# Hybrid parallel-group encoder block on one core: down's first weight slabs and the leftovers of gate and up change places, one norm and one sine chain are placed elsewhere

## The chip, the core and the metric

The kernel runs on one core of a Trainium2 chip. The metric is the device time of one execution in microseconds (us); lower is better. The times of before are those of three runs, of which the median, the lowest and the highest are given, and one more execution was recorded by the hardware profiler.

The engines by the profile's names: PE is TensorE's matmuls and PEld its weight loads, DVE is VectorE, ACT is ScalarE, POOL is GpSimd and SP is SyncE. POOL does next to no arithmetic here: it issues small transfers. SP issues the transfers that bring weights and inputs.

## The reference

One encoder block over a sequence of 256 tokens of width 2048, with a memory of 256 rows, all in f32:

```python
mem_n = rms_norm(mem, mem_norm_g)
h = rms_norm(x, norm_g[l, 0])
q, k, v, g, lr, u_f, u_h, u_s = jnp.split(h @ w_in[l], split_at, axis=-1)
y_a = gla_mixer(q, k, v, g, lr, ...)
y_b = rms_norm(fnet_mixer(u_f), grp_norm_g[l, 0])
filt = hyena_filters(feats, hy_ffn_w1[l], hy_ffn_b1[l], hy_ffn_w2[l], ...)
y_c = rms_norm(hyena_mixer(u_h, hy_conv_w[l], filt, hy_skip[l]), grp_norm_g[l, 1])
y_d = rms_norm(shortconv_mixer(u_s, sc_conv_w[l]), grp_norm_g[l, 2])
mix = jnp.concatenate([y_a, y_b, y_c, y_d], axis=-1)
x = x + mix @ w_out[l]
x = x + cross_attention(rms_norm(x, norm_g[l, 1]), mem_n, w_xq[l], w_xkv[l], w_xo[l])
x = x + swiglu(rms_norm(x, norm_g[l, 2]), w_gate_up[l], w_down[l])
return rms_norm(x, final_norm_g)
```

Each of the four mixers gives 512 of the 2048 columns of `mix`. The filters of the Hyena mixer come from a small network with two sines of 64 x 256 values. `swiglu` is `(silu(h @ w_gate) * (h @ w_up)) @ w_down` with 5632 inner columns; w_gate_up is 2048 x 11264 and w_down 5632 x 2048. These two products take the larger part of the time.

## The kernel before

**Products in three passes.** An f32 operand is split into a high part (rounded to the matmul's f32r type) and a low part (the rest). A product is high by high, low by high and high by low, so three matmuls stand where one would in plain f32. Lines L473, L474 and L475 are these three in gate, up and down, where the activations are the stationary operand and 512 columns of weights move; L422 and L423 are a pair of matmuls that does the same in the projections, with 512 and 256 moving columns.

**The stream of weights.** All weights lie in one array in the order of use, cut into slabs of 128 x 2048. SP loads a slab into a buffer `raw` (L124). Each slab has two halves of 128 x 1024. For each half ACT casts the high part `wh` (L144) and DVE subtracts to get the low part `wl` (L145). Half by half they go into pools of pairs: three buffers always, two more in gate and up (`wp2`, until the slab number `DOWN`, where down's weights begin), one more in down (`wp3`). So up to five halves, then four, are prepared ahead of their use. A slab's `raw` buffer comes free when its second half is done. One slab of down takes 24 matmuls.

**Units.** Part of gate, up and down is multiplied with seven products in place of eight (a scheme after Strassen). These parts, called units, need sums of operand blocks and of weight blocks, formed by DVE (L174 for the weights).

**Gate and up.** `mlp` (from L886) calls `gate_up`, which runs over 11 column groups j of 512 columns. At the end of each group the sums leave PSUM and `finish` (a background generator) applies silu, multiplies, transposes on DVE (`u`, L502) and stores the group to the HBM array `hidden` by eight transfers from POOL (L505). `fetch` loads `hidden` back, one row block k of 128 x 256 at a time, on POOL (L915) into buffers `tmp` (a pool of 11), and splits each into `f[k]`, the operand of down: a cast on ACT (L308) and a subtraction on DVE (L300). The row blocks are named by their number here: f14 is block 14 of 44. The tiles behind f are of several pools, so the trace shows them as `act`, `f` or others. `turn` transposes the residual x in 16 steps, each with one DVE transpose and four stores from POOL (`xrows`, L1050), and then loads it back in row form (`res`, L1054).

**The background.** `bg` is a queue of generators. Each `bg.poll()` between matmuls lets them issue some work, by an estimate of the engines' load; `bg.drain(x)` issues all that x has left at once. So the program order of all engines is the order in which Python issues instructions, and each engine works through its own in that order. A scheduler may move an instruction ahead where its inputs allow it; `mark` and `keep_place` pin a stretch to the place where it was issued. At the end of `gate_up` (L1036) three generators are drained one after the other: `end` (the last group's finish), `turned` and `early` (the fetch of f0 to f15).

**Down.** `Down` runs by a plan: first the 32 plain row blocks, in eight slabs of four blocks (`plain`, L1105), then six units of two row blocks each (`unit`, L1118) mixed with plain slabs of the second half of the columns. `ready(k)` steps the running fetch until row block k is split. `begin` (L1177) starts the second fetch, for f16 to f43, which loads six blocks ahead, and then runs the plan. The row blocks from 32 on are loaded as pairs for the units; `form` builds their sums (`e`, `s`).

**The projection behind the mixers.** `out_proj` multiplies the mixers' outputs with w_out in four parts, in the order of operands 8, 0, 4, 12 (Hyena, GLA, FNet, short convolution). Ahead of each of the last three parts it calls a function with n = 0, 1, 2, which drains the generator that makes that part's operands. `g_sc` is the norm of the short convolution: it spreads row factors over partitions with two matmuls (L398, `pm<-dgh` and `pm<-dgl`), copies the result (`rs`, L404), multiplies four tiles by it (L304) and splits them (L308, L300).

**The sine.** `sine` (L1303) is a chain of a dozen DVE operations on 64 x 256 values that reduces the argument, and one ACT sine at its end. It is called twice, for the two sine layers; the second result `hs` is the operand of the matmuls at L1400.

Of the kernel before, what the change touches and what calls it, by code (L numbers as in the profile page):

```python
# [27 lines left out]
FT = DFF // P  # L28
# [10 lines left out]
ROWS = ((0, 512), (704, 768), (880, 944), (NBLK - 48 * FT, NBLK))  # L39

LATE = 12

EARLY = 16

# [22 lines left out]
PLANS = down_plan()  # L67

DOWN = GU // 16 + 16 * DFF // 1024
# [201 lines left out]
class Block:  # L271
# [283 lines left out]
    def mixers(self):  # L555
# [77 lines left out]
        with tc.tile_pool(name="mid", bufs=1) as mid:  # L633
            self.dgp = mid
            gl = Gla(self, mid)
            with tc.tile_pool(name="hyp", bufs=1) as hyp, tc.tile_pool(name="k2", bufs=8) as k2:
                hy = Hyena(self, hyp, k2)

                mem0 = hy.piece()[:, 0:R + 16]
                nc.sync.dma_start(mem0, self.t["mem0"])  # L640
                self.bg.add(prepare(mid))

                for cols in ([0, 512], [1024], [1536]):
                    first = dict(parts=[[k] for k in range(KT)], before=start_m) if len(cols) > 1 else {}
                    for c, ps in zip(cols, self.gemm_rows("w_xkv", cols, h, **first)):
                        for r in range(2):
                            self.store_turned(self.kd[c:c + 512, r * P:(r + 1) * P], hy.piece(), ps[r][:, :])
                    if first:
                        for k in range(0, KT, 4):
                            self.load_x(k, 4)  # L650
                for hd in range(4):
                    for r, p in enumerate(self.gemm_rows("w_xkv", [D + hd * 512], h, start_x if hd == 3 else rows.append)[0]):
                        for c in range(2):
                            v, o = self.tmp(), (2 * hd + r) * 512 + c * R
                            nc.scalar.activation(v, p[:, c * R:(c + 1) * R], AF.Copy, scale=self.rcm[:, r:r + 1])
                            nc.gpsimd.dma_start(self.vd[:, o:o + R], v)
                self.bg.drain()

                def ev_u(i, p):
                    hy.feed(i, self.merge(p))  # L660
                    if i == 4:
                        self.bg.add(hy.convs())

                self.gemm("w_in", [UH + i * P for i in range(12)], h, ev_u)
                for r, p in enumerate(self.gemm_rows("w_in", [512], h, lambda k: k or low_rank())[0]):
                    nc.scalar.copy(gl.v[r], p)
                self.gemm("w_in", [256, 384, 0, 128], h, lambda i, p: gl.feed(i, self.merge(p)))
                self.gemm("w_in", scols[0:NSC], h, ev_s, narrow=True)
                self.bg.drain()

            with tc.tile_pool(name="glp", bufs=1) as glp:
                gl.open(glp)
                fn = Fnet(self, glp, act[20:24])
                g_gla = self.bg.add(gl.mix(act[4:8]))
                fn.feed(self.gemm_rows("w_in", [UF], h)[0])
                g_fn = self.bg.add(fn.mix(act[0:4], gl))
                self.gemm("w_in", scols[NSC:], h, lambda i, p: ev_s(i + NSC, p))
                g_sc = self.bg.add(self.group_norm(self.res[1], 2, act[20:24]))

                def ev_gate(i, p):  # L680
                    nc.scalar.activation(gl.gate[i], p[:, 0:R], AF.Silu)

                self.gemm("w_in", [1024 + i * P for i in range(4)], h, ev_gate, narrow=True)
                gl.done = True
                self.out_proj(lambda n: self.bg.drain((g_gla, g_fn, g_sc)[n]))

    def conv3(self, u, c, y=None):
        y = self.tmp() if y is None else y
# [188 lines left out]
    def mlp(self):  # L877
        tc, nc, act, st = self.tc, self.nc, self.act, self.st
        slots = lambda pool, n, a, b: [pool.tile([P, 512], F32R, name=f"{n}{i}") for i in range(a, b)]
        with tc.tile_pool(name="fp", bufs=1) as fp:  # L880
            self.gap(fp, 192)
            f = act[4:12] + slots(fp, "f", 8, EARLY)
            self.gap(fp, 64)
            with tc.tile_pool(name="wp2", bufs=2) as wp2, tc.tile_pool(name="rawx", bufs=1) as st.rawx, \
                    tc.tile_pool(name="sw", bufs=1) as sw, tc.tile_pool(name="gp", bufs=1) as gp:
                self.gap(sw, 192)  # L886
                st.pools.append([wp2, 2, DOWN])
                self.gate_up(sw, gp, f)
            st.pools.pop()
            st.rawx = None  # L890
            with tc.tile_pool(name="fq", bufs=1) as fq:
                self.gap(fq, 192)
                f += slots(fq, "f", EARLY, FT - 16) + self.h3
                self.gap(fq, 64)
                d = Down(self, f)
                with tc.tile_pool(name="wp3", bufs=1) as wp3, tc.tile_pool(name="sd", bufs=1) as sd:
                    self.gap(sd, 192)
                    st.pools.append([wp3, 1, max(UNITS) + 1])
                    d.begin(sd)
                st.pools.pop()  # L900
                with tc.tile_pool(name="hp", bufs=1) as hp:
                    self.gap(hp, 192)
                    held = [hp.tile([P, 512], F32R, name=f"held{i}") for i in range(HELD // 2)]
                    st.places = list(zip(held[0::2], held[1::2]))
                    d.end()
# [24 lines left out]
    def gate_up(self, sw, gp, f):  # L930

        nc, st = self.nc, self.st
# [71 lines left out]
        turned = self.bg.add(self.turn())  # L1004
        early = end = None
        for j in range(DFF // 512):
# [3 lines left out]
            if j == 1:  # L1010
                early = self.bg.add(self.fetch(f, 0, EARLY, 3, 2.0))
# [22 lines left out]
                            self.bg.poll()  # L1034
            self.bg.drain(last)
            end = self.bg.add(finish(j, cs, s))  # L1036
        for x in (end, turned, early):
            self.bg.drain(x)

    def turn(self):  # L1040

# [20 lines left out]
class Down:  # L1062
# [39 lines left out]

    def plain(self, c, i, k0):
        for k in range(k0, k0 + 4):
            self.ready(min(FT, k + 3))  # L1105
            w = self.st.take("w_down", k, (c + i) * 512, 4)
            if c + i == 3 and k >= PLAIN - LATE:
                self.held.append((k, w))
                continue
            for r in range(2):  # L1110
                self.part((i, r), *self.whole(k, r), *w)
# [3 lines left out]

    def unit(self, c, k):

        self.ready(k + 2)  # L1118
        formed = lambda n: [self.forms[k][:, a + n * P:a + (n + 1) * P] for a in (0, 384)]
        for (key, a), w in zip((("p1", self.whole(k, 0)), ((1, 0), formed(2)), ((0, 0), self.whole(k + 1, 0)),  # L1120
                                ("p5", self.whole(k, 1)), ("p7", formed(1)), ("p6", formed(0)), ((0, 1), self.whole(k + 1, 1))),
                               self.st.take_forms("w_down", (k, k + 1), c * 512, c * 512 + 512), strict=True):
            self.part(key, *a, *w)
# [44 lines left out]
    def run(self, c, plan, other):  # L1168
        for n, x in enumerate(plan):
# [4 lines left out]
                self.banks.update({n: other() for n in ("p1", "p5", "p7", "p6")})  # L1174
            self.unit(c, x[1])

    def begin(self, sd):  # L1177

        b = self.b
        self.sd = sd  # L1180
        self.fetching = b.bg.add(b.fetch(self.f, EARLY, FT, 6, SOON, self.form))
        one, two = PLANS
        n, self.rest = (1 + max(i for i, x in enumerate(plan) if x[0] == "unit") for plan in PLANS)
        self.open(one, b.bank)
        self.run(0, one[:n], b.gbank)
        todo = [b.bg.add(self.combine(0))]
        self.run(0, one[n:n + 1], None)
        b.bg.drain(todo[0])
        todo.append(b.bg.add(self.settle(0, self.both(0))))
        self.run(0, one[n + 1:], None)  # L1190
        b.bg.drain(todo[1])
        last = b.bg.add(self.settle(1, self.both(1)))
        self.open(two, b.gbank)
        self.run(2, two[:1], None)
        b.bg.drain(last)
        self.run(2, two[1:self.rest], b.bank)
        last = b.bg.add(self.combine(2))
        self.run(2, two[self.rest:self.rest + 1], None)
        b.bg.drain(last)
# [48 lines left out]
class Hyena:  # L1248
# [57 lines left out]
    def sine(self, p, bias):  # L1306

        b, nc = self.b, self.b.nc
        a, n = b.tmp()[0:64, :], b.tmp()[0:64, :]
        v = lambda c: b.vec[0:64, c:c + 1]  # L1310
        ts = lambda out, in0, s1, op0, s2=None, op1=None: nc.vector.tensor_scalar(
            out=out, in0=in0, scalar1=s1, scalar2=s2, op0=op0, **({} if op1 is None else {"op1": op1}))
        b.bg.dve(6 * 200, 6)
        ts(a, p, v(bias), ALU.add)
        ts(a, a, v(V_FR), ALU.mult)
        ts(n, a, 1.0 / (2 * math.pi), ALU.mult)
# [3 lines left out]
            b.stt(a, n, -c, a, ALU.mult, ALU.add)  # L1320
        ts(a, a, PI_LO, ALU.min, -PI_LO, ALU.max)
        nc.scalar.activation(a, a, AF.Sin)
        return a

    def triple(self, p, th, tl, hi, lo, start, stop):
# [501 lines left out]
```

## Time and profile before

| quantity | value |
|---|---|
| median of three runs | 1464.77 us (1464.11 to 1465.36) |
| the profiled execution, its own time | 1465.34 us |
| span in the profile | 1463.4 us |
| mean granted clock of TensorE | 0.995 |
| instructions | 19727 |
| ACT busy | 843.3 us, 58% |
| DMA traffic | 307.16 MB, mean 210 GB/s |

The span is the time from the first to the last recorded instruction; the device time has 1.9 us more around it. A busy share is a mean over stages with different limits. The page's groups name a line, an engine, an operation and its tiles; a timeline lists the instructions of one engine in order of start, joining equal neighbours (x4), with the idle time ahead of them in brackets and what ended it. Times in a timeline count from the start of the span. The views used further on are the page, the waits of TensorE, the windows of 40 us, timelines of single engines around 476 us and 1216 to 1270 us, and the transfers issued in short stretches.

### The profile page before, as it was taken

The page shows a single profiled execution, that of the slowest core. Times are in us where ns is not written, and L with a number is a line of the kernel's source. Part 1 is how long each engine was busy: PE and PEld are TensorE (multiplying, and loading weights), DVE is VectorE, ACT ScalarE, POOL GpSimd, SP SyncE. Part 2 cuts the span into 40 slices and gives each one's busy share as a digit, 9 for nine tenths or more (in the row PEclk, how much of TensorE's full clock was granted, in tenths as well). Part 3 has the DMA queues.
Part 4 walks back from the last instruction along what each step waited for, and adds up shares of the span by engine and source line. Part 5 has one row for each costly group of instructions (what it writes and reads, how often), then busy time and mean ns, then how long its engine had stood idle before and what let it go on. Part 6 is the DMA issues. An engine that isn't in the chain of part 4 may idle for free.

```text
span 1463.4 us, 19727 instructions
## 1 busy us (share of the span) xinstructions
PE 1443.8 (99%) x7219; PEld 1220.3 (83%) x7219; DVE 1193.2 (82%) x1748; ACT 843.3 (58%) x1250; POOL 171.6 (12%) x294
## 2 busy tenths in 40 slices
PE   9999999999999999999999999999999999999997
PEld 7878888898899788888888888888888887788886
DVE  6588768778867767777778999999999996898875
ACT  6555655566656546765655555555555554665554
POOL 0220100000000001110003345111001113200000
PEclk9999999999999999999999999999999999999999
DMA  9975564454535455545556768666556656565654
GB/s 348 350 256 208 203 214 160 157 185 155 201 125 211 173 193 206 188 173 176 199 186 224 258 231 276 224 210 222 207 210 245 218 201 218 207 222 183 227 202 144
DMA packets 57393, 307.16 MB, mean 210 GB/s; under 512 B 9773, under 2 KB 11470, under 8 KB 25680
## 3 DMA queue, kind: packets, MB, share of 16 engines
q1 hardware_dynamic: 45920, 281.11, 54.0%
q0 software_dynamic: 10944, 24.14, 5.5%
q8 instruction: 56, 0.92, 0.2%
q10 hardware_dynamic: 432, 0.66, 0.1%
q14 instruction: 41, 0.34, 0.1%
HBM read 291.71 MB, written 14.16 MB: 209 GB/s over the span
## 4 chain that ended last, share of the span: by engine, by line
PE 94%; DVE 2%; issue 1%; DMA 1%; ACT 1%; POOL 0%; SPq 0%; DVEq 0%; POOLq 0%; ACTq 0%
PE pg L422 19%; PE pg L474 13%; PE pg L475 13%; PE pg L473 13%; PE pg L423 10%; PE pm L475 6%; PE pm L473 6%; PE pm L474 6%; DVE wl L145 1%; PE pm L1328 1%; PE pg L419 1%; PE pg L420 1%; DMA tmp<-hidden 1%; PE pm L870 1%; PE pm L843 1%
## 5 line engine op out<-in xcount | busy, mean ns | idle before, releaser
L144 ACT CAST wh<-raw 128x1024 fp32r<-128x1024 f32 (+1 forms) x589 | 590.3, 1013 | 477.4 <-PE pg L475 154.9
L145 DVE TENSOR_TENSOR wl<-raw,wh 128x1024 fp32r<-128x1024 f32 (+1 forms) x589 | 684.1, 1178 | 185.3 <-ACT wh L144 178.6
L422 PE MATMUL pg<-act,wh 128*128 128x512 f32 x1104 | 390.3, 395 | 2.9 <-DVE act L300 2.9
L423 PE MATMUL pg<-act,wl 128*128 128x256 f32 x1216 | 341.8, 281 | 0.0
L474 PE MATMUL pg<-wl,act 128*128 128x512 f32 (+1 forms) x689 | 268.5, 390 | 2.1 <-DVE wl L145 2.1
L473 PE MATMUL pg<-wh,act 128*128 128x512 f32 (+1 forms) x689 | 268.8, 391 | 0.0
L475 PE MATMUL pg<-wh,act 128*128 128x512 f32 (+1 forms) x689 | 268.5, 390 | 0.0
L422 PEld LDWEIGHTS pg<-act,wh 128*128 128x128 f32 x1104 | 208.6, 189 | 48.7 <-DVE act L300 3.3
L423 PEld LDWEIGHTS pg<-act,wl 128*128 128x128 f32 x1216 | 229.8, 189 | 0.8 <-DVE wl L145 0.5
L474 PEld LDWEIGHTS pg<-wl,act 128*128 128x128 f32 x689 | 129.8, 188 | 30.1 <-DVE wl L145 3.3
L473 PEld LDWEIGHTS pg<-wh,act 128*128 128x128 f32 x689 | 129.7, 188 | 27.6 <-issue 0.8
L475 PEld LDWEIGHTS pg<-wh,act 128*128 128x128 f32 x689 | 129.7, 188 | 27.4 <-issue 0.4
L474 PE MATMUL pm<-wl,act 128*128 128x512 f32 x318 | 124.6, 392 | 3.1 <-DVE wl L145 3.1
L475 PE MATMUL pm<-wh,act 128*128 128x512 f32 x318 | 124.6, 392 | 1.1 <-DVE act L300 1.1
L473 PE MATMUL pm<-wh,act 128*128 128x512 f32 x318 | 124.1, 391 | 0.0
L174 DVE TENSOR_TENSOR raw<-raw 128x1024 f32<-128x1024 f32 x129 | 112.0, 868 | 3.0
L505 POOL DMA_DIRECT2D hidden<-u x88 | 56.7, 652 | 284.5 <-DVE u L502 261.1
L474 PEld LDWEIGHTS pm<-wl,act 128*128 128x128 f32 x318 | 60.0, 189 | 16.1 <-DVE wl L145 3.5
L475 PEld LDWEIGHTS pm<-wh,act 128*128 128x128 f32 x318 | 60.1, 189 | 14.2 <-DVE act L300 1.7
L473 PEld LDWEIGHTS pm<-wh,act 128*128 128x128 f32 x318 | 60.0, 189 | 12.5
L1050 POOL DMA_DIRECT2D xrows<-tmp x64 | 36.9, 585 | 144.3 <-DVE rc L304 126.6
L300 DVE TENSOR_TENSOR tmp<-pg,tmp 128x256 f32<-128x256 f32 x78 | 32.5, 419 | 5.4 <-ACT tmp L429 4.6
(353 smaller groups left out, 1762.0 us busy)
## 6 DMA issues: line engine op xcount, KB each, us to landing
raw<-in_W SPq DMA_DIRECT2D x246, 1024.0 KB, 4.9
raw<-in_W SPq DMA_DIRECT2D x11, 512.0 KB, 7.9
hidden<-u POOLq DMA_DIRECT2D x88, 64.0 KB, 4.3
tmp<-hidden POOLq DMA_DIRECT2D x44, 128.0 KB, 5.1
res<-in_xT SPq DMA_DIRECT2D x8, 512.0 KB, 8.3
k<-in_mem SPq DMA_DIRECT2D x8, 256.0 KB, 7.1
k<-in_x SPq DMA_DIRECT2D x8, 256.0 KB, 9.5
keys<-k POOLq DMA_DIRECT2D x32, 64.0 KB, 5.4
```

What stands on the lines that cost most here:

```text
L144: nc.scalar.copy(wh[:, a:b], r[:, a:b])
L145: nc.vector.tensor_tensor(out=wl[:, a:b], in0=r[:, a:b], in1=wh[:, a:b].bitcast(F32), op=ALU.subtract)
L174: op = lambda out, a, b, what=ALU.subtract: nc.vector.tensor_tensor(out=out, in0=a, in1=b, op=what)
L300: self.nc.vector.tensor_tensor(out=out, in0=a, in1=b, op=op)
L419: self.nc.tensor.matmul(p[:, 0:R], wh, slot[:, 0:R], start=start, stop=False)
L422: self.nc.tensor.matmul(p[:, :], wh, slot[:, :], start=start, stop=False)
L423: self.nc.tensor.matmul(p[:, 0:R], wl, slot[:, 0:R], start=False, stop=stop)
L473: self.nc.tensor.matmul(p, hi, wh, start=start, stop=False)
L474: self.nc.tensor.matmul(p, hi, wl, start=False, stop=False)
L475: self.nc.tensor.matmul(p, lo, wh, start=False, stop=stop)
L505: nc.gpsimd.dma_start(to[:, :, 32 * a:32 * a + 32], u[32 * a:32 * a + 32, :].rearrange("f (b t) -> f b t", t=32))
L1050: nc.gpsimd.dma_start(to[:, :, c:c + 32], u[32 * a:32 * a + 32, :].rearrange("t (b f) -> t b f", f=32))
```

## The change

Four places are touched.

- In `out_proj`'s function the norm of the short convolution is drained one part sooner: with FNet's mix, ahead of FNet's part, and no longer ahead of its own.
- `gate_up` no longer drains its three leftovers but returns them. A new method `Down.start` opens down's plan, runs its first two slabs (`AHEAD`), with the buffers of gate and up still open for two slabs more, and drains the leftovers behind them. `begin` goes on from the third slab.
- `ready` in `plain` and `unit` asks for row blocks further ahead: `k + 4` in place of `k + 3`, limited by the length of f at that time, and `k + 4` in place of `k + 2`.
- `sine` pins its chain at the place where it is issued.

```diff
+AHEAD = 2
...
-                self.out_proj(lambda n: self.bg.drain((g_gla, g_fn, g_sc)[n]))
+                self.out_proj(lambda n: [self.bg.drain(g) for g in ((g_gla,), (g_fn, g_sc), ())[n]])
...
-                st.pools.append([wp2, 2, DOWN])
-                self.gate_up(sw, gp, f)
+                st.pools.append([wp2, 2, DOWN + AHEAD])
+                d = Down(self, f)
+                d.start(*self.gate_up(sw, gp, f))
...
-                d = Down(self, f)
...
-        for x in (end, turned, early):
-            self.bg.drain(x)
+        return end, turned, early
...
-            self.ready(min(FT, k + 3))
+            self.ready(min(len(self.f), k + 4))
...
-        self.ready(k + 2)
+        self.ready(min(FT, k + 4))
...
+    def start(self, end, turned, early):
+
+        b = self.b
+        self.fetching = early
+        self.open(PLANS[0], b.bank)
+        self.run(0, PLANS[0][:AHEAD], None)
+        for x in (end, turned, early):
+            b.bg.drain(x)
...
-        self.open(one, b.bank)
-        self.run(0, one[:n], b.gbank)
+        self.run(0, one[AHEAD:n], b.gbank)
...
         b.bg.dve(6 * 200, 6)
+        mark = b.mark()
         ts(a, p, v(bias), ALU.add)
...
         nc.scalar.activation(a, a, AF.Sin)
+        b.keep_place(mark)
         return a
```

## The prediction

> **What bounds the kernel now.** I read the page first: where the busy time lies and whether the clock of TensorE holds.
>
> ```profile
> PE 1443.8 (99%) x7219; PEld 1220.3 (83%) x7219; DVE 1193.2 (82%) x1748; ACT 843.3 (58%) x1250; POOL 171.6 (12%) x294
> PEclk9999999999999999999999999999999999999999
> ```
>
> TensorE is busy for 1443.8 of the span's 1463.4 us, so no edit outside the matmuls can win more than the 19.6 us of idle time and what a lowered clock adds. The waits of TensorE, longest total first, say where the idle time is:
>
> ```profile
> PE pm L474 <- DVE wl L145: 3.1, 1, 3.1
> PE pg L422 <- DVE act L300: 2.9, 1, 2.9
> PE pm L475 <- DVE act L300: 1.1, 1, 1.1
> ```
>
> Each is one single wait (second number). The windows of 40 us place them; columns are the stretch, its sum, then busy us of PE (instructions), PEld, DVE, ACT, POOL, the granted clock, the DMA share and GB/s:
>
> ```profile
> 440.00:480.00 40.00, 37.01 (x261) 34.44 (x262) 31.76 (x77) 23.95 (x44) 2.71 (x5) 0.98 0.56 198
> 480.00:520.00 40.00, 40.00 (x219) 35.05 (x218) 28.07 (x47) 22.48 (x39) 0.00 (x0) 0.94 0.50 176
> 1200.00:1240.00 40.00, 36.88 (x156) 30.02 (x155) 29.56 (x42) 20.64 (x32) 12.83 (x22) 0.96 0.64 217
> 1240.00:1280.00 40.00, 38.92 (x170) 31.36 (x169) 34.14 (x62) 26.35 (x45) 9.21 (x17) 1.00 0.61 214
> ```
>
> The reader is to see two holes, one near 476 us (2.99 idle, clock 0.98 and then 0.94) and one near 1222 us (3.12 idle, clock 0.96), and a smaller one of 1.08 behind 1240. The first is the norm of the short convolution in out_proj; the others are the passage from gate and up into down. The change works on both.
>
> **Part A, the norm one part sooner (lambda at L684).** The columns of a timeline are start, duration, engine, line, operation, output<-inputs, and in brackets the idle time ahead.
>
> ```profile
> 470.35 0.39 PE L422 MATMUL pg<-act,wh 128*128 128x512 f32 x1
> ...
> 475.21 0.28 PE L398 MATMUL pm<-dgh,ones 128*128 128x256 f32 x1
> ...
> 476.03 0.28 PE L423 MATMUL pg<-act,wl 128*128 128x256 f32 x1
> 479.25 0.79 PE L422 MATMUL pg<-act,wh 128*128 128x512 f32 x1 [2.95 <-DVE act L300]
> ...
> 485.13 0.40 PE L422 MATMUL pg<-act,wh 128*128 128x512 f32 x1
> ```
>
> ```profile
> 475.65 0.37 ACT L404 COPY rs<-pm 128x256 f32<-128x256 f32 x1 [1.34 <-PE pm L398]
> ...
> 477.18 1.32 ACT L308 CAST act<-res 128x256 fp32r<-128x256 f32 x4
> ```
>
> ```profile
> 467.17 0.61 DVE L304 SCALAR_TENSOR_TENSOR dgl<-ident,rc,dgh 128x128 fp32r<-128x128 f32 x2
> ...
> 476.05 1.68 DVE L304 SCALAR_TENSOR_TENSOR res<-res,vec,rs 128x256 f32<-128x256 f32 x4 [0.49 <-ACT rs L404]
> 477.64 1.22 DVE L145 TENSOR_TENSOR wl<-raw,wh 128x1024 fp32r<-128x1024 f32 x1
> 478.78 1.43 DVE L300 TENSOR_TENSOR act<-res,act 128x256 fp32r<-128x256 f32 x4
> ```
>
> The last four operands (act, L300) hang on a chain: the two L398 matmuls that spread the row factors, the copy rs, four multiplications, a cast and a subtraction each. In program order those two matmuls move ahead by 14 pairs of L422/L423. A pair is (475.21 − 470.35)/14 = 0.347 us, so they stand at 470.35; what they read was done at 467.78. ACT, free then but for a weight cast, copies rs by 472.1. DVE has a weight half of 1.22 in hand, so the multiplications lie at about 473.0 to 474.5, and the first operand is split at 474.9. One weight half follows and the other three come at 476.4, 476.7 and 477.05. TensorE, with no hole, asks for the four at 476.38, 476.73, 477.08 and 477.42: the first is 1.5 early, the others about 0.35. Without stall its nine pairs (18 matmuls) to the next normal one end at 476.38 + 9 × 0.347 = 479.51, and before that matmul starts at 485.13: **5.6 us**, of which 2.87 is the stall and 2.75 the slow pace after it. On the other queues, SP issues the last load of x one weight load sooner and that weight load about 1 us earlier than before; nothing is lost there. If the margin of 0.35 is gone by a microsecond, 0.6 is given back. Bounds: 4.6 to 5.7. The waits name no other wait of TensorE up to the second hole that this would push into, so the gain is carried there.
>
> The Trainium skill, "TensorE: Matmul & The Clock Gate", section "What's actually happening", puts the fall to half clock after an idle window of about 3.4 us that runs freely. Taken as a threshold the 2.95 would have cost no clock and part A would be worth 2.9; the trace shows 0.63 us a matmul after it, so the measured row decides.
>
> **The sine chain (L1303 mark).** Only the second chain moves: it now stands as one block behind the row factors.
>
> ```profile
> 92.79 0.42 DVE L300 TENSOR_TENSOR hs<-tmp,hs 64x256 fp32r<-64x256 f32 x1
> ```
>
> ```profile
> 103.43 0.58 PE L1400 MATMUL pm<-w3h,hs 128*128 128x512 f32 x1
> ```
>
> Its result, ready at 93.2, is asked for at 103.43. Moved behind some four weight halves it comes near 99: 4 us of cover remain. Cost 0; if the cover went, each us late would be a us of TensorE.
>
> **Part B, two slabs of down ahead of the leftovers.**
>
> ```profile
> 1216.17 0.39 PE L473 MATMUL pm<-wh,act 128*128 128x512 f32 x1
> ...
> 1221.61 0.61 PE L473 MATMUL pm<-wh,act 128*128 128x512 f32 x2
> 1225.34 0.50 PE L474 MATMUL pm<-wl,act 128*128 128x512 f32 x1 [3.12 <-DVE wl L145]
> ...
> 1229.33 0.39 PE L473 MATMUL pm<-wh,act 128*128 128x512 f32 x1
> ...
> 1265.36 0.49 PE L475 MATMUL pm<-wh,act 128*128 128x512 f32 x1 [1.08 <-DVE act L300]
> ...
> 1266.38 0.39 PE L473 MATMUL pg<-wh,act 128*128 128x512 f32 x1
> ```
>
> ```profile
> 1219.19 1.30 DVE L502 STREAM_TRANSPOSE u<-h 128x512 f32<-128x512 f32 x2
> ...
> 1224.06 3.50 DVE L145 TENSOR_TENSOR wl<-raw,wh 128x1024 fp32r<-128x1024 f32 x3
> ...
> 1268.66 4.09 DVE L145 TENSOR_TENSOR wl<-raw,wh 128x1024 fp32r<-128x1024 f32 x4
> ```
>
> ```profile
> 1216.37 1.05 ACT L144 CAST wh<-raw 128x1024 fp32r<-128x1024 f32 x1 [0.59 <-PE pg L475]
> ```
>
> Slab 0 runs from 1216.17 to 1221.61, 24 matmuls, 0.227 each. Slab 1's first low half (L145 at 1224.06) stood behind the leftovers on DVE although its cast was done at 1217.4. Now both slabs come first: the stall of 3.12 goes, and with it the slow pace (10 matmuls in 1229.33 − 1225.34 = 3.99 for 2.27, so 1.72). Eight plain slabs at 5.44 would end at 1259.7; the first unit began at 1266.38, so the passage loses 6.7 in all today, and that is the most part B could win.
>
> What is late next: the leftovers. Their transposes move behind the three low halves (3.50) and two transposes of `turn`, about 4 us. Their stores stand at the head of POOL's queue, and behind them everything down still has to fetch:
>
> ```profile
> 1213.87 0.56 POOL L915 DMA_DIRECT2D tmp<-hidden  x1 [6.05 <-DVE act L300]
> 1220.19 5.16 POOL L505 DMA_DIRECT2D hidden<-u  x8 [5.76 <-DVE u L502]
> 1225.35 4.36 POOL L915 DMA_DIRECT2D tmp<-hidden  x8
> ```
>
> ```profile
> L1050 POOL DMA_DIRECT2D xrows<-tmp x64 | 36.9, 585 | 144.3 <-DVE rc L304 126.6
> ```
>
> The stores now run 1224.2 to 1229.3; four stores of `turn` (0.585 each, last row) take POOL to 1231.7, and only there is row block f14 loaded, which before was loaded at 1213.87. How long a load takes has two ends, by the issues of three short stretches (1251.2 to 1253.4, 1255.6 to 1258, 1261.4 to 1263; the last number is us to landing):
>
> ```profile
> raw<-in_W SPq DMA_DIRECT2D x1, 1024.0 KB, 5.9
> tmp<-hidden POOLq DMA_DIRECT2D x2, 128.0 KB, 5.5
> ```
>
> ```profile
> tmp<-hidden POOLq DMA_DIRECT2D x4, 128.0 KB, 2.4
> ```
>
> ```profile
> tmp<-hidden POOLq DMA_DIRECT2D x2, 128.0 KB, 3.2
> ```
>
> Close behind a weight load it is 5.5, alone 2.4, in between 3.2. f14 lands at 1234.1 to 1237.2, and its split stands behind a weight half (1.05 and 1.22): ready at 1237 to 1238. TensorE asks at 1216.17 + 3.5 × 5.44 = 1235.2: a new wait of about 2.4, between 0 and 3.3.
>
> Then f18 and f19 stand behind four more stores of `turn` and two loads that wait for them: issued near 1237.5, landed 1240 to 1243; the second half of slab 5, behind f19's cast on ACT, ends on DVE at t0 = 1242.7 to 1245.7, middle 1244.2. From there each step waits for the one before, whatever TensorE does. Splitting f21 frees a buffer for f32; f32's form stands before the next low half on DVE; f24 frees f35's buffer, whose cast stands before the cast of slab 7's second half on ACT (before: behind it); f28 frees f41's, whose cast stands before the unit's second weight half (before: behind it). Each of these loads is issued about 0.6 behind a weight load, because the half that ends also frees the raw buffer. Three links of 0.6 + 5.5 and 12.0 of conversions (casts of 1.05 and subtractions of 1.22 with the splits between: 1.4 for the half whose cast is already done, then 2.5, 2.5, 3.0 and 2.5) put the unit's fourth low half at 1244.2 + 18.3 + 12.0 = 1274.5. Before, it is the first of the four at 1268.66 and ends at 1269.8. So the upper value is +4.7; with 1245.7 for t0 it is +6.2. With all three loads landing in 2.4 it would be −4.6, and TensorE then decides: plain slabs end at 1259.7 + 2.4 = 1262.1, against 1266.38, −4.3. I take two links long and the last, furthest from the crowded start, at the 3.2 of the row: 2.3 less, **+2.4**. The clock that the new wait might lower lies ahead of this chain and is covered by it.
>
> Part B removes 4.84 at slab 1 and pays it back and more on the way to the first unit.
>
> **The sum.** −5.6 (A) + 0 (sine) + 2.4 (B) = −3.2 against the profiled execution's 1465.34 (span 1463.4 and 1.9 around it): 1462.1. That execution lies 0.57 above the median of the runs, 1464.77, so 1461.6.
>
> **The rivals.** (1) *The loads land early, and B wins too.* For it: the 2.4 of the loads that follow no weight load. Against it: the chain ties loads and weight loads together. It gives B between −4.3 and 0: 1454.9 to 1459.2.
>
> By the Trainium skill, "DMA: Bandwidth & Descriptors", section "Issuing engines are not separate DMA queues", transfers of different engines run on the same 16 DMA engines and interleave. With fair interleaving a load of 128 KB would meet only as much of the weight load, an estimate of 2.9 us from the rows above (2.4 plus 3.5 × 128/1024), and B would be near −3; the row of 5.5 beside 5.9 says that it lands almost with the weight load, and I follow the row.
>
> (2) *All three links are long:* B +4.7 to +6.2, 1463.9 to 1465.4, no change that can be told. For it: 5.5 in the row; against it: 3.2 for f41 today.
>
> (3) *Slower: the unit starves.* One mechanism at the first unit: TensorE has done the plain slabs near 1262 and its second weight half is delayed by f41's cast; once that single wait passes about 2.95, the clock falls as at 479.25 and the unit, whose low halves DVE delivers just in time, starts slow (2.75, the larger price seen). It needs the late t0 as well: −5.6 + 6.2 + 2.75 = +3.4, 1468.1. Against it: TensorE's waits there come in pieces, one for each row block.
>
> (4) *Part A gains only the stall* because rs meets a busy ACT: −2.9 + 2.4, 1464.3.
>
> **How the numbers follow.** The forecast with its own range (B +0.3 to +4, 1459.5 to 1463.2) has 0.44, rival 1 0.24, rival 2 0.15, rival 3 0.12, rival 4 0.05. A measurement can tell 0.2%, 2.9 us, from no change: faster is below 1461.84, slower above 1467.7. Of the forecast's 0.44, 0.24 lies below 1461.84; with rival 1 that makes faster 0.48. Slower is rival 3 and its neighbours, 0.13; same 0.39. The range reaches over most of rival 1 and all of rival 2: 1456.0 to 1467.2.
>
> **What would show it.** Right for A: no wait at L422 near 476, a window 480 to 520 with clock 1.00. Right for B: no wait at L474 near 1222; f14's load behind the stores of `turn` on POOL; a new wait of TensorE for act or f near 1235; the unit's fourth low half ending near 1266.6 on the clock of the trace (1269.8 + 2.4 − 5.6). Wrong would be: a wait of 1 us or more at L398's operands; loads that land in 2.4 throughout (rival 1); a clock under 1.00 between 1260 and 1280 (rival 3); a wait at L1400 (sine).

## The result and the profile after

The kernel after takes 1466.78 us (median of 20 runs, 1465.18 to 1469.29), the kernel before 1464.51 us in the same series (20 runs, 1461.96 to 1465.99). The ratio is 1.0016, 95% interval 1.0009 to 1.0023: 2.3 us slower, less than the 0.2% set as the bound for a change that can be told. The forecast was 1461.6, with 1456.0 to 1467.2 as its range: the time lies in the range, but it moved the other way.

The profiled execution has a span of 1464.7 us, 1.3 more than before. First TensorE's busy time on its page:

```profile
PE 1442.2 (98%) x7219; PEld 1217.2 (83%) x7219; DVE 1192.9 (81%) x1748; ACT 842.9 (58%) x1250; POOL 171.5 (12%) x294
```

and its longest waits by what it waited for (us in total, times, longest):

```profile
PE pg L476 <- DVE wl L147: 4.0, 4, 1.6
PE pm L475 <- ACT f L310: 3.2, 2, 1.8
PE pm L477 <- DVE f L302: 2.9, 2, 2.7
```

The lines named here are two higher than before: L475, L476, L477 are what L473, L474, L475 were, L146 and L147 the weight casts and subtractions, L302 and L310 the splits, L917 the fetch. The 3.1 for wl in pm and the 2.9 for act in pg have gone, as forecast. In their place stand waits for row blocks, 3.2 for their casts and 2.9 for their subtractions. Before, the matmuls into pg waited this long for low halves:

```profile
PE pg L474 <- DVE wl L145: 2.1, 2, 1.6
```

Those 2.1 lay ahead of 440 us. Of the 4.0 now, 1.8 lie there too, and 2.2 are new, in the first unit of down. The windows say where the idle time stands:

```profile
440.00:480.00 40.00, 39.96 (x282) 37.26 (x281) 32.52 (x79) 25.55 (x47) 2.71 (x5) 1.00 0.61 207
480.00:520.00 40.00, 40.00 (x232) 35.24 (x232) 31.02 (x50) 23.50 (x41) 0.00 (x0) 1.00 0.57 196
1200.00:1240.00 40.00, 36.54 (x159) 29.25 (x158) 27.65 (x44) 18.46 (x32) 19.06 (x34) 1.00 0.68 227
1240.00:1280.00 40.00, 33.66 (x134) 25.40 (x133) 30.39 (x58) 21.41 (x40) 8.61 (x16) 0.96 0.54 192
```

Between 440 and 520 TensorE is idle for 0.04 us and the clock is 1.00. From 1200 to 1240 the idle time is 3.46 (before 3.12), and from 1240 to 1280 it is 6.34 (before 1.08): 9.8 in place of 4.2, all on the way from gate and up into the first unit. TensorE's rows there begin with the first matmul of down,

```profile
1209.91 0.39 PE L475 MATMUL pm<-wh,act 128*128 128x512 f32 x1
```

and go on with those that had to wait, and the first of the unit (1263.79):

```profile
1230.89 0.50 PE L475 MATMUL pm<-wh,f 128*128 128x512 f32 x1 [1.78 <-ACT f L310]
...
1238.60 0.50 PE L475 MATMUL pm<-wh,f 128*128 128x512 f32 x1 [1.46 <-ACT f L310]
...
1250.22 0.57 PE L477 MATMUL pm<-wh,f 128*128 128x512 f32 x1 [2.72 <-DVE f L302]
...
1263.79 0.39 PE L475 MATMUL pg<-wh,act 128*128 128x512 f32 x1
...
1268.87 0.50 PE L476 MATMUL pg<-wl,act 128*128 128x512 f32 x1 [1.36 <-DVE wl L147]
```

Slab 0 starts at 1209.91, 6.3 earlier than the 1216.17 of before (0.4 of it stood already ahead of the norm: the row factors' low half started at 466.81 here, at 467.17 before), and there is no stall at slab 1. Then 1.78, 1.46 and 2.72 are lost on the row blocks f14, f18 and f24 (six matmuls for each row block, counted from 1209.91). The unit still begins sooner, at 1263.79 against 1266.38, but its own low halves are late (1.36 at 1268.87, and more on either side). What was won by 1210 is spent by 1272.

The chain behind it, on ACT:

```profile
1238.14 0.72 ACT L310 CAST f<-tmp 128x256 fp32r<-128x256 f32 x2 [6.37 <-DMA tmp<-hidden]
1238.77 1.04 ACT L146 CAST wh<-raw 128x1024 fp32r<-128x1024 f32 x1
...
1248.77 0.41 ACT L310 CAST act<-tmp 128x256 fp32r<-128x256 f32 x1 [5.22 <-DMA tmp<-hidden]
...
1255.24 0.41 ACT L310 CAST act<-tmp 128x256 fp32r<-128x256 f32 x1 [3.05 <-DMA tmp<-hidden]
...
1263.19 0.41 ACT L310 CAST act<-tmp 128x256 fp32r<-128x256 f32 x1 [3.72 <-DMA tmp<-hidden]
1263.51 1.04 ACT L146 CAST wh<-raw 128x1024 fp32r<-128x1024 f32 x1
```

Each time ACT stands before the cast of a row block whose load has not landed (6.37, 5.22, 3.05, 3.72 us), and right behind it in its queue stands the cast of a weight half (L146, shown for the first and the last; the other two begin at 1249.08 and 1255.56) that needs nothing from that load. DVE gets its halves late in the same rhythm:

```profile
1239.84 1.23 DVE L147 TENSOR_TENSOR wl<-raw,wh 128x1024 fp32r<-128x1024 f32 x1 [0.51 <-ACT wh L146]
...
1248.41 0.29 DVE L302 TENSOR_TENSOR e<-tmp 128x128 f32<-128x128 f32 x1 [4.86 <-DMA tmp<-hidden]
1248.62 1.22 DVE L147 TENSOR_TENSOR wl<-raw,wh 128x1024 fp32r<-128x1024 f32 x1
...
1256.63 1.22 DVE L147 TENSOR_TENSOR wl<-raw,wh 128x1024 fp32r<-128x1024 f32 x1 [2.37 <-ACT wh L146]
...
1264.58 1.23 DVE L147 TENSOR_TENSOR wl<-raw,wh 128x1024 fp32r<-128x1024 f32 x1 [2.37 <-ACT wh L146]
...
1270.08 3.49 DVE L147 TENSOR_TENSOR wl<-raw,wh 128x1024 fp32r<-128x1024 f32 x3
```

And POOL, which issues the loads:

```profile
1225.20 0.58 POOL L917 DMA_DIRECT2D tmp<-hidden  x1
1227.17 1.64 POOL L917 DMA_DIRECT2D tmp<-hidden  x3 [1.39 <-DMA hidden<-u]
...
1231.92 3.23 POOL L917 DMA_DIRECT2D tmp<-hidden  x6
...
1243.51 1.08 POOL L917 DMA_DIRECT2D tmp<-hidden  x2 [0.72 <-DVE f L302]
1250.46 1.08 POOL L917 DMA_DIRECT2D tmp<-hidden  x2 [5.88 <-DVE f L302]
...
1258.49 1.08 POOL L917 DMA_DIRECT2D tmp<-hidden  x2 [3.45 <-DVE act L302]
```

f14 is loaded at 1225.20 (first row), f15 to f17 at 1227.17, f18 to f23 at 1231.92, all behind stores or loads of the residual; the load of f18 took 6.2 us by the issues between 1231.9 and 1232.3, beside a load of the residual that took 6.4:

```profile
res<-xrows POOLq DMA_DIRECT2D x1, 256.0 KB, 6.4
tmp<-hidden POOLq DMA_DIRECT2D x1, 128.0 KB, 6.2
```

Later each pair of loads waits for DVE to free a buffer (the 5.88 and 3.45 in brackets end with DVE).

### The profile page after: what moved, and what is told of

Same layout as the page of the kernel before. It is cut to its first block, busy times and chain, and to the rows that moved or that the text cites. A ratio compares the mean times of both kernels' runs of the same rounds, so it can differ in the third digit from the quotient of the medians.

```text
span 1464.7 us, 19727 instructions
## 1 busy us (share of the span) xinstructions
PE 1442.2 (98%) x7219; PEld 1217.2 (83%) x7219; DVE 1192.9 (81%) x1748; ACT 842.9 (58%) x1250; POOL 171.5 (12%) x294
## 4 chain that ended last, share of the span: by engine, by line
PE 93%; DMA 2%; DVE 2%; POOL 1%; issue 1%; ACT 1%; SPq 0%; POOLq 0%; ACTq 0%; DVEq 0%
PE pg L424 18%; PE pg L476 13%; PE pg L477 13%; PE pg L475 13%; PE pg L425 10%; PE pm L477 6%; PE pm L476 6%; PE pm L475 6%; DMA tmp<-hidden 1%; PE pm L1339 1%; DVE wl L147 1%; PE pg L421 1%; PE pg L422 1%; PE pm L872 1%; PE pm L845 1%
## 5 line engine op out<-in xcount | busy, mean ns | idle before, releaser
L146 ACT CAST wh<-raw 128x1024 fp32r<-128x1024 f32 (+1 forms) x589 | 590.4, 1013 | 469.6 <-PE pg L477 154.3
L147 DVE TENSOR_TENSOR wl<-raw,wh 128x1024 fp32r<-128x1024 f32 (+1 forms) x589 | 683.5, 1175 | 178.4 <-ACT wh L146 171.6
L476 PE MATMUL pg<-wl,act 128*128 128x512 f32 (+1 forms) x689 | 268.3, 389 | 3.3 <-DVE wl L147 3.2
L475 PE MATMUL pg<-wh,act 128*128 128x512 f32 (+1 forms) x689 | 268.4, 390 | 0.5 <-ACT wh L146 0.5
L477 PE MATMUL pg<-wh,act 128*128 128x512 f32 (+1 forms) x689 | 268.2, 389 | 0.0
L476 PEld LDWEIGHTS pg<-wl,act 128*128 128x128 f32 x689 | 129.4, 188 | 31.8 <-DVE wl L147 5.1
L475 PEld LDWEIGHTS pg<-wh,act 128*128 128x128 f32 x689 | 129.3, 188 | 28.2 <-issue 0.8
L477 PEld LDWEIGHTS pg<-wh,act 128*128 128x128 f32 x689 | 129.3, 188 | 27.3 <-issue 0.4
L477 PE MATMUL pm<-wh,act 128*128 128x512 f32 x318 | 123.9, 390 | 0.7 <-DVE act L302 0.6
L475 PE MATMUL pm<-wh,act 128*128 128x512 f32 x318 | 123.8, 389 | 0.0
L476 PE MATMUL pm<-wl,act 128*128 128x512 f32 x318 | 123.7, 389 | 0.0
L477 PEld LDWEIGHTS pm<-wh,act 128*128 128x128 f32 x318 | 59.7, 188 | 13.8 <-DVE act L302 1.5
L475 PEld LDWEIGHTS pm<-wh,act 128*128 128x128 f32 x318 | 59.7, 188 | 12.6 <-ACT act L310 0.3
L476 PEld LDWEIGHTS pm<-wl,act 128*128 128x128 f32 x318 | 59.7, 188 | 12.4
L475 PE MATMUL pm<-wh,f 128*128 128x512 f32 x80 | 32.1, 401 | 3.2 <-ACT f L310 3.2
```

Source lines behind the costliest of these rows:

```text
L146: nc.scalar.copy(wh[:, a:b], r[:, a:b])
L147: nc.vector.tensor_tensor(out=wl[:, a:b], in0=r[:, a:b], in1=wh[:, a:b].bitcast(F32), op=ALU.subtract)
L475: self.nc.tensor.matmul(p, hi, wh, start=start, stop=False)
L476: self.nc.tensor.matmul(p, hi, wl, start=False, stop=False)
L477: self.nc.tensor.matmul(p, lo, wh, start=False, stop=stop)
```

## The experiments

The table shows the runs that combine the parts of the change, x for a part that is in the kernel; "residual early" is an edit of the experiments, told below. All ratios are to the kernel before, which ran beside each kernel on the same chip; us are the difference of the ratio from 1 times 1464.5.

| run | norm | slabs first | look-ahead k + 4 | residual early | median us | ratio (95%) | us |
|---|---|---|---|---|---|---|---|
| before | | | | | 1464.51 | 1 | 0 |
| after | x | x | x | | 1466.78 | 1.0016 (1.0009 to 1.0023) | +2.3 |
| e1_norm_only | x | | | | 1458.52 | 0.9961 (0.9948 to 0.9973) | −5.7 |
| e2_no_norm | | x | x | | 1471.05 | 1.0048 (1.0035 to 1.0060) | +7.0 |
| e3_ready_old | x | x | | | 1460.60 | 0.9975 (0.9965 to 0.9984) | −3.7 |
| e7_ready_new | | | x | | 1470.35 | 1.0039 (1.0025 to 1.0052) | +5.7 |
| e8_turn_early | x | x | | x | 1454.80 | 0.9936 (0.9922 to 0.9949) | −9.4 |
| e11_after_turn_early | x | x | x | x | 1460.58 | 0.9968 (0.9955 to 0.9980) | −4.7 |
| e18_norm_turn | x | | | x | 1459.59 | 0.9962 (0.9950 to 0.9975) | −5.6 |

**Part A alone and the change without it.**

```diff
-self.out_proj(lambda n: self.bg.drain((g_gla, g_fn, g_sc)[n]))
+self.out_proj(lambda n: [self.bg.drain(g) for g in ((g_gla,), (g_fn, g_sc), ())[n]])
```

> The kernel before with only the norm of the short convolution drained one part sooner. My theory (the change's cost lies all in down): part A is worth 5.6 us by itself, so 1464.5 - 5.6 = about 1458.9, no wait near 476 us, and the hole of 3.1 us in down's slab 1 as before. Rival (the gain of A is paid back later whatever down does, as the later stages are bound by their transfers): 1463 or more, with new idle time of TensorE behind 490 us.

> The kernel after, but with the norm drained where it was before, so down's part and the sine alone. My theory: both parts add, so 1466.8 + 5.6 = about 1472.4, 7 to 8 us slower than before. Rival (down's part loses only because A made it start earlier against transfers that come at their own pace): about 1466 to 1468, within 1 to 2 us of the kernel after.

Part A alone gives −5.7 us, and without it the rest costs +7.0: apart they add to +1.3, together they measure +2.3, the same within their intervals. The rival, a gain paid back whatever down does, is out.

**The look-ahead taken back, and alone.** The kernel after with

```diff
-self.ready(min(len(self.f), k + 4))
+self.ready(min(len(self.f), k + 3))
...
-self.ready(min(FT, k + 4))
+self.ready(k + 2)
```

> The kernel after with the two look-aheads of down as before (k + 3 in plain, k + 2 in unit); slabs first, norm and sine as in the kernel after. Theory 1 (the deeper look-ahead puts casts and forms that wait for loads ahead of weight halves on ACT and DVE; that is what costs): the waits for f35 and f41 no longer hold the weight halves, 4 us less than the kernel after, about 1462.5. Theory 2 (the leftovers that stand behind the first slabs, with the stores and loads of the transposed residual on POOL's queue, cost it, wherever the casts stand): within 1 us of 1466.8.

and the kernel before with `k + 4` in both places:

> The kernel before with only the deeper look-ahead of down (k + 4 in plain, k + 4 in unit). Theory 1: f41's cast stands ahead of the unit's second weight half here too, so 2 to 4 us slower than before, 1466.5 to 1468.5. Theory 2: the loads come early enough in the order of before, 1464 to 1465.5, no change.

The first falls from +2.3 to −3.7 us, the second is 5.7 slower than the kernel before, by the look-ahead alone. Theory 1 holds in both. Its price was 6.0 and 5.7 where 4 and 2 to 4 were expected. On ACT the run e7_ready_new shows the same queue as the kernel after, with its slabs where they were before:

```profile
1252.81 0.41 ACT L308 CAST act<-tmp 128x256 fp32r<-128x256 f32 x1 [2.85 <-DMA tmp<-hidden]
1253.12 1.04 ACT L144 CAST wh<-raw 128x1024 fp32r<-128x1024 f32 x1
...
1259.12 0.41 ACT L308 CAST act<-tmp 128x256 fp32r<-128x256 f32 x1 [2.90 <-DMA tmp<-hidden]
1259.43 1.04 ACT L144 CAST wh<-raw 128x1024 fp32r<-128x1024 f32 x1
...
1267.16 0.41 ACT L308 CAST act<-tmp 128x256 fp32r<-128x256 f32 x1 [3.81 <-DMA tmp<-hidden]
1267.47 1.04 ACT L144 CAST wh<-raw 128x1024 fp32r<-128x1024 f32 x1
```

Three casts wait 2.85, 2.90 and 3.81 for a load, and each has a weight half behind it. These are row blocks of the units, from f32 on; no cast of a plain row block waits for its load in this passage. Without the look-ahead (e3_ready_old) TensorE has two long waits in this passage:

```profile
1230.90 0.50 PE L475 MATMUL pm<-wh,f 128*128 128x512 f32 x1 [3.02 <-ACT f L310]
...
1251.91 0.50 PE L477 MATMUL pm<-wh,f 128*128 128x512 f32 x1 [2.32 <-DVE f L302]
```

The first is for f13, by the count of matmuls: with the shallower look-ahead the fetch stands one block further back than in the kernel after, where this wait is for f14 and was forecast at 2.4. The second is for f25, which stands on DVE behind the form of f32 and f33.

**Plain's look-ahead alone.** The kernel before, with `k + 4` in `plain` and `k + 2` in `unit`.

> The kernel before with only plain's look-ahead at k + 4; unit's stays k + 2. Theory: plain's step forces the splits and the forms ahead of the weight halves, unit's adds nothing, so 1470 as with both (e7_ready_new, 1470.35). Rival (unit's look-ahead makes the wait for f41 and so half of the price): 1466 to 1468.

1469.70 us, ratio 1.0033 (1.0020 to 1.0045): plain's one step gives the price that both have together. The unit's two steps add nothing that these intervals could show. Not run was `k + 4` limited to the plain row blocks; it would tell whether the earlier forms for the unit are the whole price, as the rows of e7_ready_new suggest.

**The leftovers' order.** The kernel after with `for x in (end, early, turned)`:

> The kernel after with the leftovers drained in the order finish, fetch, turn, so that f14 to f19 no longer stand behind the last stores and loads of the transposed residual on POOL's queue; deep look-ahead as in the kernel after. My theory has two terms in down: the late start of the loads and the chain of loads that the deep look-ahead makes. Here only the first is lighter: t0 some 3 us earlier and f14 in time, so 1462 to 1464. Rival (the chain alone decides, the start is set by the landing of the last hidden stores): 1466 to 1467, as the kernel after.

1466.20 us, ratio 1.0014 (1.0005 to 1.0023), no gain. It does not settle what it was made for: the trace shows the second round of the residual's stores at 1232.04 on POOL all the same, ahead of the loads from f16 on, and TensorE waits 2.46 for a row block at 1237.13, so the start was not made lighter, only rearranged.

**The residual out of the way.** In `gate_up`, ahead of the last group's finish, on the kernel of e3_ready_old:

```diff
             self.bg.drain(last)
+            if j == DFF // 512 - 1:
+                self.bg.drain(turned)
             end = self.bg.add(finish(j, cs, s))
```

> The look-aheads as before, first slabs ahead of the leftovers, norm sooner, and the transposed residual's rest drained before the last group's finish, so that behind the first slabs only the finish and the fetch are left. Theory: the wait for f14 of 3.0 us and the slow clock behind it go or shrink to 1, so 1460.6 - 3 to 4.5 = 1456 to 1457.6. Rival (f14 lands late because of the weight loads and the hidden stores ahead of it, not because of the residual's stores): 1459.5 to 1461.

1454.80 us, the ratio 0.9936: 3.9 parts in a thousand, 5.7 us, below e3_ready_old, more than expected. Its windows (busy us of PE second):

```profile
1200.00:1240.00 40.00, 40.00 (x179) 33.11 (x177) 31.84 (x50) 21.98 (x40) 16.66 (x29) 1.00 0.74 259
1240.00:1280.00 40.00, 38.25 (x165) 30.45 (x164) 37.66 (x65) 26.37 (x41) 5.42 (x10) 1.00 0.53 192
```

and its loads and stores on POOL:

```profile
1217.42 5.18 POOL L507 DMA_DIRECT2D hidden<-u  x8 [1.18 <-DVE u L504]
1222.59 2.76 POOL L917 DMA_DIRECT2D tmp<-hidden  x5
1226.61 1.08 POOL L917 DMA_DIRECT2D tmp<-hidden  x2 [1.26 <-DMA hidden<-u]
```

TensorE is busy for all 40 us from 1200 to 1240. POOL goes from the last eight hidden stores (5.18) straight back to loads, and of the waits for plain row blocks 0.16 for f29 and 1.59 for f31, the last, remain. The same edit on the kernel after, and on the kernel with the norm alone:

> The kernel after, deep look-ahead kept, with the transposed residual's rest drained before the last group's finish. It differs from e8_turn_early (1454.8) by the look-ahead alone. If the look-ahead's price is a chain of loads that holds weight halves, whatever starts it: about 6 us more than e8_turn_early, 1460 to 1461.5. Rival (the chain costs only when the loads start late): 1454.5 to 1456.5.

> The kernel before with the norm sooner and the residual's rest drained early, down's slabs not ahead. It differs from e8_turn_early by the first slabs alone (and the sine). Theory: the stall of 3.1 at slab 1 and what slow clock follows stay, so 1457 to 1458.5, about 3 us slower than e8_turn_early: the slabs ahead are worth what the prediction said once nothing else stands on POOL's queue. Rival (early residual is the whole gain): 1454.5 to 1455.5.

With the look-ahead (e11) it is 4.7 us slower than e8_turn_early: the chain costs even where the loads start early. Its ACT rows:

```profile
1242.79 0.41 ACT L310 CAST act<-tmp 128x256 fp32r<-128x256 f32 x1 [2.81 <-DMA tmp<-hidden]
...
1249.14 0.41 ACT L310 CAST act<-tmp 128x256 fp32r<-128x256 f32 x1 [2.98 <-DMA tmp<-hidden]
...
1257.05 0.41 ACT L310 CAST act<-tmp 128x256 fp32r<-128x256 f32 x1 [3.67 <-DMA tmp<-hidden]
```

2.81, 2.98 and 3.67, close to those of e7_ready_new. Without the slabs ahead (e18) the residual's early rest gains nothing (−5.6 against −5.7 of e1_norm_only), and the slabs ahead are then worth 0.9962 − 0.9936 = 0.0026 by the ratios, 3.8 us. (The medians of 1459.59 and 1454.80 differ by 4.8, but come from different chips.) The traces agree with 3.8: from down's first matmul to the first of the unit it takes 50.25 us in e18_norm_turn and 46.40 in e8_turn_early. The forecast had 4.84 for the stall and the slow pace at slab 1.

**The first form, and the sine.** Plain's look-ahead cut to the plain row blocks (`min(PLAIN, k + 3)`), with the norm alone and on e8_turn_early:

> The kernel before with the norm sooner, and with plain's look-ahead limited to the plain row blocks, so that the first form for a unit (which waits for f32 and f33) is no longer forced ahead of the last plain slab's weight halves. If the remaining wait of 2.0 us of TensorE for f31 is made by that form on DVE, it goes and the time is 1458.5 - 2 = about 1456.5. Rival (the unit needs the same loads anyway, so the wait moves into the unit): 1458 to 1459.5.

> The edits of the two runs before this one together (residual drained early, look-ahead limited to the plain row blocks, first slabs ahead, norm sooner). If both of their terms are won and add: 1453.5 to 1455.5, the fastest of all. Rival (the unit's loads then decide): 1457 to 1459.

1459.54 us (0.9964, 0.9951 to 0.9976) and 1454.72 us (0.9932, 0.9919 to 0.9944): no different from 1458.52 and 1454.80. By the times the rival holds. The traces show it in part. The wait of 2.0 in e1_norm_only was for f25, by the count of matmuls, not for f31. In e9_form_late it is gone, and TensorE's idle time from 1240 to 1280 falls from 3.09 to 1.77. But a wait of 0.57 for a low half is new inside the unit, and from the unit's first matmul to the end of the span it takes 197.8 us in place of 196.6. The slow pace behind the stall at slab 1, too, took 1.6 where e1_norm_only's took 0.2 (the last section shows how that varies). Whether the later form is worth something stays open. e10_both and e8_turn_early are the fastest kernels here, 9.4 to 10 us below the kernel before.

The sine chain pinned in the kernel before:

> The kernel before with only the sine chain pinned to its place. Expected: no change, 1464 to 1465; the second chain has about 4 us of cover ahead of the matmuls that read it. Rival (the block of DVE work delays a weight half and with it TensorE): 0.5 to 2 us more, with a new wait for wl between 85 and 105 us.

1464.65 us, ratio 1.0000 (0.9991 to 1.0009), as expected.

## Why the prediction was wrong

**Right in its mechanism, its size partly luck.** Part A: forecast 5.6, measured 5.7 (interval 4.0 to 7.6). In the kernel after, rs stands thus on ACT

```profile
471.08 0.37 ACT L406 COPY rs<-pm 128x256 f32<-128x256 f32 x1
```

and the last three splits on DVE

```profile
475.41 1.09 DVE L302 TENSOR_TENSOR act<-res,act 128x256 fp32r<-128x256 f32 x3
```

rs is done at 471.45 (forecast 472.1) and the last splits at 476.50, with TensorE's first of the four asked for near 476 and the last a microsecond later; no wait is recorded. The sine: 0. Its result on DVE in the kernel after

```profile
98.09 0.42 DVE L302 TENSOR_TENSOR hs<-tmp,hs 64x256 fp32r<-64x256 f32 x1
```

and its first use on TensorE

```profile
103.03 0.58 PE L1411 MATMUL pm<-w3h,hs 128*128 128x512 f32 x1
```

leave 4.5 us of cover; 99 and 4 were forecast.

The luck is in the 2.75 of slow pace, which was read from one trace. Five kernels here keep the norm in its old place, and all stall for 2.94 or 2.95 near 476 us. From the row factors' low half (`dgl`) to down's first matmul the kernel before takes 749.0 us, e7_ready_new and e12_plain_deep 747.7 and 747.9, e2_no_norm and e14_sine_only 746.3. In the last two no slow pace followed the stall. With the norm sooner it is 743.1 in all nine traces. So the gain up to down was 5.9, 4.6, 4.8 or 3.2 us, 4.3 in the mean of the five, and the forecast took the largest. Where the rest of the measured 5.7 lies is not shown; 4.3 is inside its interval.

The stall at slab 1 is gone, and e18_norm_turn against e8_turn_early gives its worth once nothing takes it back: 3.8 us, where 4.84 was forecast. f14 stood behind the residual's stores, and the wait for it came: 1.78 and 0.21 at the end of the chain that was worked out with 2.4.

**Wrong: the term of part B.** It was set at +2.4 and measured at about +7 (e2_no_norm +7.0; in the spans +1.3 with 5.7 won by A). Rival 2's mechanism is what happened, and further out than its upper end. The chain itself was worked out right: from t0 to the unit's fourth low half 18.3 + 12.0 = 30.3 was the sum. In the trace t0 is the end of the half at 1239.84, 1241.07, and the fourth low half, the first of the three joined in the row at 1270.08, ends at about 1271.2: 30.1. That the sums agree so closely is partly luck: f32's load was issued 1.1 us behind t0 and not 0.6, and took 6.2, while the other two took 4.8 and 4.7, where 5.5 was reckoned for each. Two choices inside it failed:

- *"I take two links long and the last, furthest from the crowded start, at the 3.2 of the row: 2.3 less".* The last load, issued at 1258.49, was cast at 1263.19, 4.7 later; the links, from the end of one half to the landing, took 7.3 (1241.07 to 1248.41), 5.4 (1249.84 to 1255.24) and 5.3 (1257.85 to 1263.19), together 18.0 against 18.3 with all three long. The 2.3 were not there.
- *"middle 1244.2"* for t0. f18's load was issued at 1231.92; the forecast, moved by A's 5.7, has f19 at 1231.8. But it landed after 6.2 us where the middle of 2.4 and 5.5 had been taken. On the clock of the kernel before t0 is 1241.07 + 5.7 = 1246.8, 2.6 later.

Together 4.9; added to +2.4 they make +7.3, close to what the runs show for part B.

**Not weighed at all: which edit makes the chain.** The prediction told that f35's and f41's casts now stand ahead of weight halves that had been ahead of them, and put it to the slabs that come first. The runs put it to the look-ahead: `k + 4` in place of `k + 3` in `plain` alone costs 4.8 us (e12), and both steps together 4.7 to 6.0 (e7 +5.7, after against e3 +6.0, e11 against e8 +4.7), with or without the first slabs. It was left without a price of its own, as a part of B. The traces also say where it is paid: mostly behind the unit's first matmul, where the low halves are late. From there to the end of the span it takes 200.0 to 201.9 us in the six traces with the deeper look-ahead and 196.5 to 197.8 in the eight without. The slabs ahead are worth −3.8 with POOL's queue clear, and nothing with the residual's stores in it, where the row blocks from f13 or f14 to f19 come late: +2.1 by the ratios of e3_ready_old and e1_norm_only (0.9975 and 0.9961), whose intervals overlap. So the small change in time hides three terms: −5.7 for the norm, +6 for the look-ahead, and 0 to +2 for slabs ahead of a blocked queue.

**The rivals.** Rival 1, early loads, is out: the loads of the chain landed 4.7 to 6.2 after issue. (The 2.9 estimated under it is 2.8 by its own terms; nothing hung on it.) Rival 3 did not come in its form: the waits inside the unit are 1.36 at most, and from 1260 to 1280 the granted clock is 1.00. The clock did fall, to 0.50 from 1250.51 to 1253.93, but ahead of the unit and behind a wait of only 2.72 (at 1250.22), so 2.95 was no threshold. Rival 4's mechanism is out: rs was done at 471.45, sooner than forecast. Its size, the stall alone, is what part A won against the two traces without a slow pace.

## What to carry to other kernels

Asking a queue in order for an operand earlier than its load can land gives nothing to the operand and takes the time from everything queued behind it: a look-ahead is right when the load has landed at the point of the request, and asking too far ahead cost 5 to 6 us here. When work is put off, look at which queue it stands at the head of later, and clear that queue first: the same two slabs gained 4 us with the queue clear and nothing without. Price each edit of a change by itself, do not take the slow pace behind a stall from one trace, and where a chain is worked out step by step, take its own sum before one that looks milder.

## What the hardware showed that was not expected

The same stall of 3.1 us at down's slab 1 cost very different slow stretches behind it. In e1_norm_only the clock did not fall there, in e7_ready_new it fell at once. The matmul behind the stall and the next one, in e1_norm_only

```profile
1220.60 0.50 PE L474 MATMUL pm<-wl,act 128*128 128x512 f32 x1 [3.11 <-DVE wl L145]
1220.94 0.40 PE L475 MATMUL pm<-wh,act 128*128 128x512 f32 x1
```

and the same rows in e7_ready_new:

```profile
1223.95 0.79 PE L474 MATMUL pm<-wl,act 128*128 128x512 f32 x1 [3.12 <-DVE wl L145]
1224.55 0.63 PE L475 MATMUL pm<-wh,act 128*128 128x512 f32 x1
```

From the matmul behind the stall to the fourteenth after it, 14 × 0.227 = 3.17 at full pace, it took 3.35 in the one (1220.60 to 1223.95) and 5.97 in the other (1223.95 to 1229.92), so 0.2 and 2.8 lost; the kernel before lost 1.7. In e3_ready_old the slow pace (0.63 a matmul) began only at the seventh matmul, 1.5 us behind a wait of 3.02. So 1.7 for it was one value out of this spread.

The traces show what the spread hangs on. In each of them the changes of the granted clock lie whole multiples of 3.413 us apart; a stretch at half clock lasts 3.41 (before, 1225.74 to 1229.16) or 6.83 (e7_ready_new, 1222.88 to 1229.71). Cut each span into pieces of 3.41 us at these points, from 12 us on. At full clock, every piece of the fourteen traces in which TensorE is idle for 1.9 us or more is followed by half clock, none with 1.75 or less is, and between them one with 1.80 is and two with 1.82 and 1.85 are not. A piece at half clock is followed by another where it holds 1.03 us of idle time or more, and not where it holds 0.49 or less. So a stall near 3 us is a draw: it depends on how the cuts fall. The 2.95 near 476 put 2.41 into one piece in e12_plain_deep, and the clock halved; in e14_sine_only it was parted into 1.75 and 1.19, and the clock held. The 3.11 of e1_norm_only was parted into 1.47 and 1.65.

The Trainium skill, "TensorE: Matmul & The Clock Gate", section "What's actually happening", has a window of this length that runs freely, which fits. It puts the fall behind a whole idle window of about 3.4 us, which does not fit: 1.9 to 2.0 us of idle time inside one piece were enough here.
